# A hybrid encoder layer on one core: pacing of two top-k searches, earlier attention logits, FFN products on another engine

## The chip, the cores and the metric

The kernel runs on one core of a Trainium2 chip. Its time is the device time of one execution in microseconds (us). A core has TensorE (PE, matrix products and transposes into PSUM), VectorE (DVE), ScalarE (ACT), GpSimd (POOL, no access to PSUM) and SyncE (SP), which here only issues transfers. Each engine works through its own instruction list in order and waits on semaphores of the others.

## The reference

One layer of a trunk on x of 2048 rows x 1024, all in float32, with three groups of heads between two norms and a gated FFN behind them:

```python
h = rmsnorm(x, g1)
p = h @ w_in
hA = mlstm_chunkwise(...)
hB = rglru(causal_conv4(lx)) * gelu(lg)
hC = dsa_attention(q, k, v, iq, ik, iw)
x = x + rmsnorm(concat(hA, hB, hC) @ w_out, g2)
u = causal_conv3(rmsnorm(x, g3) @ ffn_up)
gate, up = split(u)
x = x + rmsnorm((gelu(gate) * up) @ ffn_down, g4)
```

In `dsa_attention` an indexer scores every admissible key for every query, the 256 highest are kept, and four heads attend to those keys alone.

## The kernel before, in words

**Stages.** Rows go in four blocks of 512 (`b`). The mixer does, block by block, the input projections, the mLSTM, the LRU, and starts the attention. The FFN then goes over the same four blocks, while the attention's later row tiles still run beside it. Inside FFN block b (`ffn`, L1027) the output projection of block b+1 (`out_proj`, L945) stands in front of the last but one group of products; block 0's stands in the mixer.

**Products.** A float32 product is three products of halves: `gemm_t` and `gemm_r` (L254, L270) go over pieces of weights, each a high part `wh` and a remainder `wl`, loaded on SP's queue or made from a raw load on ACT and POOL (L208, L214). Results lie in four PSUM banks `mm`; three banks `sd` serve everything else, one bank `av` the attention's result.

**Order.** PE's order is the program's (a manual schedule), the other engines' instructions are ordered by the framework's own estimate of time. The program holds a clock `self.now` of PE's work (L48). After each chunk of a product `tick` (L95) runs at most one step of the background streams (generators; the number that a step yields is the time until the next is due), in the order norm, gates, lru, mlstm, att, score. `lanes` (L78) runs the steps of two top-k searches: lane 0 takes the even row tiles (128 queries) and counts on DVE, lane 1 the odd ones and counts on ACT, with a few whole-row DVE steps at its beginning, middle and end. A lane's step sets its own next due time: the yielded length x 1.7 (L93). Lane steps have low priority and are kept behind the last marked DVE and ACT instructions (`dmark`, `amark`).

**Search.** `dsa_mask` (L767) looks for the 256th highest score of n = 128(i+1) keys: a 15-step bisection over the upper 16 bits of the score, a 16-step one over the lower, then a mask of additive values. On DVE a step is a count (L705), a comparison (L717) and a candidate update (L719); on ACT it is a sum of signs (L727) and two small activations. A search holds two of four `pl` planes, the finished mask one, so tile i+2's search begins when tile i's attention is over (L81, L929). Scores of tile i also wait for the mask of tile i-2 (L668).

**Attention.** `dsa_att` (L831) has `nch` chunks of 512 keys, one for tiles 0 to 3 up to four for 12 to 15. `scores(h, ci)` loads keys `ks`, makes logits in an `sd` bank, adds the mask and takes the maximum on DVE into `L` (four buffers, L852); with the head's last chunk it scales the maximum (L859) and exponentiates the head's chunks on ACT (L864). `turn` transposes a chunk of `L` on PE (L59) and copies it to `PT` (L875), `values` multiplies it by the values `vs`. `scores` runs one head ahead of `turn`:

```python
for h in range(4):
    for ci in range(nch):
        turn(h, ci)
        if h < 3:
            scores(h + 1, ci)
        ...
        yield 3.5 if ci + 1 < nch else 4.5
```

`need(b)` (L932) runs all steps of the attention up to block b before `out_proj(b)` reads `d_cat`, without other products between them.

**FFN.** 22 pairs of products (gate and up) go in groups `(4, 4, 4, 4, 4, 2)`, in the last block `(4, 4, 4, 5, 5)`. `conv3` (L1014) reads PSUM once on ACT and twice on DVE (L1020) into `cu` (four buffers); then Gelu on ACT, the product on DVE (L1045), its high part on ACT (L1048), the remainder on DVE (L1049). A group's down product (L1073) comes after the next group's first pair; after a group of five and after the last it comes at once.

**Small things.** `row_rstd` (L130) adds the two halves of a sum of squares and scales it on one column (L144, L145). `proj_val` (L395) and `proj_mlstm` (L415) copy projections out of PSUM; those of `v` all on ACT (L400, L437).

Of the kernel before, what the change touches and what calls it, by code (L numbers as in the profile page):

```python
# [21 lines left out]
EPS = 1e-6  # L22
# [15 lines left out]
class Trunk:  # L38
# [39 lines left out]
    def lanes(self, force=None):  # L78
        for n, lane in enumerate(self.lane):
            while lane and (lane[0][1] <= self.now or force == n):  # L80
                if lane[0][2] and self.planes > 2:  # L81
                    break
                self.planes += 2 * lane[0][2]
                lane[0][2] = False
                with ExitStack() as c:
                    c.enter_context(self.tc.issue_after(self.dmark.ins))
                    c.enter_context(self.tc.issue_after(self.amark.ins))
                    c.enter_context(self.tc.high_priority(offset=-LOW))
                    lag = next(lane[0][0], None)
                if lag is None:  # L90
                    lane.pop(0)
                else:
                    lane[0][1] = max(lane[0][1], self.now - 4.0) + lag * LANES[n]  # L93

# [35 lines left out]
    def row_rstd(self, srcs, first=False):  # L130
        nc = self.nc
        n = len(srcs)
        ss = self.sm.tile([128, n, 2], F32, name="ss")
        for i, x in enumerate(srcs):
            for j in range(2):
                if first and j:
                    c = x[:, 512:1024]
                    junk = self.lp.tile([128, T], F32, name="jk", tag="lt")
                    nc.vector.tensor_tensor_reduce(junk, c, c, 1.0, 0.0, OP.mult, OP.add, ss[:, i, 1:2])
                    continue  # L140
                junk = self.sm.tile([128, 512], BF, name="junk", bufs=1)
                nc.scalar.activation(junk, x[:, j * 512:(j + 1) * 512], AF.Square, accum_out=ss[:, i, j:j + 1])
        v = self.sm.tile([128, n], F32, name="var")
        nc.vector.tensor_tensor(v, ss[:, :, 0], ss[:, :, 1], OP.add)  # L144
        nc.vector.tensor_scalar(v, v, 1.0 / D, EPS, OP.mult, OP.add)  # L145
        return self.rsqrt(self.sm, v, [128, n], "rs")

    def norm_load(self, src, b):
# [246 lines left out]
    def proj_val(self, b, h):  # L395
        nc = self.nc
        o = self.gemm_r(self.win((C_AV, 256)), h)
        for i in range(4):
            vt = self.mst.tile([128, 256], F32, name="vt", tag="mst")
            nc.scalar.activation(vt, o[i][:, :256], AF.Copy)  # L400
            nc.scalar.dma_start(self.d_v[:, :, 4 * b + i, :], vt.rearrange("p (h d) -> p h d", h=4))

    def proj_qk(self, b, h, seen=None):
# [11 lines left out]
    def proj_mlstm(self, b, h, nm):  # L415
        nc = self.nc
        for c0, col in ({"o": (C_MO, 772), "q": (C_MQ, 0), "k": (C_MK, 0), "v": (C_MV, 384)}[nm],):
            if nm == "q":
                o = self.gemm_t(self.win((c0, 384)), [128] * 3, h)
                for i in range(3):  # L420
                    t = self.mst.tile([128, T], F32, name="mst")
                    if i % 2:
                        self.dmark = nc.vector.tensor_copy(t, o[i])
                    else:
                        self.amark = nc.scalar.activation(t, o[i], AF.Copy)
                    nc.scalar.dma_start(self.d_q[i * 128:(i + 1) * 128, b * T:(b + 1) * T], t)
                continue
            n = 392 if nm == "o" else 384
            o = self.gemm_r(self.win((c0, n)), h)
            w = 388 if nm == "v" else 384  # L430
            gs = []
            for i in range(4):
                t = self.mst.tile([128, T], F32, name="mst")
                if nm == "v":
                    tv = t[:, :388].rearrange("p (h d) -> p h d", h=MH)
                    nc.gpsimd.memset(tv[:, :, 96:97], 1.0)
                    self.amark = nc.scalar.activation(tv[:, :, 0:96], o[i][:, :384].rearrange("p (h d) -> p h d", h=MH), AF.Copy)  # L437
                elif nm == "o":
                    self.amark = nc.scalar.activation(t[:, :384], o[i][:, :384], AF.Sigmoid)
                    g = self.mst.tile([128, 8], F32, name="mg", bufs=8)  # L440
                    nc.vector.tensor_copy(g, o[i][:, 384:392])
                    gs.append(g)
                elif i % 2:
                    self.dmark = nc.vector.tensor_copy(t[:, :384], o[i][:, :384])
                else:
                    self.amark = nc.scalar.activation(t[:, :384], o[i][:, :384], AF.Copy)
                r0 = b * T + i * 128
                nc.scalar.dma_start(self.d_m[r0:r0 + 128, col:col + w], t[:, :w])
            if nm == "o":
                self.spawn("gates", self.gates(b, gs), 3.0)  # L450
# [258 lines left out]
    def bisect(self, junk, src, n, need, top):  # L709
# [4 lines left out]
        while bit >= 1:  # L714
            cnt = yield from self.count(junk, src, n, c[:, 0:1])
            t = self.small("stp")
            ve.tensor_scalar(t, cnt, need[:, 0:1], -float(bit), OP.is_lt, OP.mult)  # L717
            c2 = self.small("cand")
            ve.scalar_tensor_tensor(c2, t, float(bit // 2), c, OP.add, OP.add)  # L719
            c = c2  # L720
            bit //= 2
            yield 0.4
# [21 lines left out]
    def bisect_act(self, junk, src, n, need, top):  # L744
# [7 lines left out]
        while True:  # L752
# [8 lines left out]
                yield 0.8 + 0.00084 * n  # L761
                continue
            yield 3.0 + 0.00084 * n
            ve.scalar_tensor_tensor(c, t, 0.5, nb, OP.mult, OP.subtract)
            return c

    def dsa_mask(self, i, sc):  # L767
# [8 lines left out]
        count, bisect = (self.count_act, self.bisect_act) if a else (self.count, self.bisect)  # L776
        u = 0.3 + 0.0011 * n
        ve.tensor_copy(hi[:, :n], halves(I16, 1))
        yield u
        c0 = yield from count(lo.bitcast(BF), hi, n, 0.0)  # L780
        neg, m16, need = s1("neg"), s1("m16", I16), s1("need")
        ve.tensor_scalar(neg, c0, float(TOPK), None, OP.is_lt)
        ve.tensor_scalar(m16, neg, -1.0, None, OP.mult)
        ve.tensor_tensor(need, c0, neg, OP.mult)
        ve.tensor_scalar(need, need, -1.0, float(TOPK), OP.mult, OP.add)  # L785
        ve.tensor_scalar(hi[:, :n], hi[:, :n], m16[:, 0:1], None, OP.bitwise_xor)
        yield 0.8 + u
# [5 lines left out]
        ve.tensor_tensor(need2, need, cg, OP.subtract)  # L793
        ve.tensor_scalar(lo[:, :n], halves(U16, 0), mu, None, OP.bitwise_xor)
        yield u
        ve.scalar_tensor_tensor(lo[:, :n], hi[:, :n], F[:, 0:1], lo[:, :n], OP.is_equal, OP.mult)
        yield u
# [4 lines left out]
        ve.tensor_tensor(need3, need2, cg, OP.subtract)  # L802
        ve.tensor_scalar(need3, need3, -BIG, None, OP.mult)
# [5 lines left out]
        yield 0.8  # L809
        ve.tensor_scalar(lt[:, :n], sc[:, :n], tf, -BIG, OP.is_lt, OP.mult)  # L810
        yield u
        ve.tensor_scalar(eq[:, :n], sc[:, :n], tf, -BIG, OP.is_equal, OP.mult)
        yield u
        ve.tensor_tensor_scan(sc[:, :n], eq[:, :n], eq[:, :n], 0.0, OP.add, OP.min)
        yield 0.3 + 0.0013 * n
        ve.scalar_tensor_tensor(eq[:, :n], sc[:, :n], need3[:, 0:1], eq[:, :n], OP.is_lt, OP.mult)
        yield u
# [13 lines left out]
    def dsa_att(self, i):  # L831
# [50 lines left out]
                self.mm(av[p0:p0 + 64, h * 128:(h + 1) * 128], vs[:, k, :], pt[:, k * 128:(k + 1) * 128],  # L882
                        4 * ci + k < 2, 4 * ci + k >= nk - 2)
        yield 4.0
        for ci in range(nch):
            scores(0, ci)
            yield 1.5 if ci + 1 < nch else 4.0
        av = self.ps.tile([128, 512], F32, name="av", bufs=1)
        before = None
        for h in range(4):  # L890
            for ci in range(nch):
                turn(h, ci)
                if h < 3:
                    scores(h + 1, ci)
                if before is not None:
                    values(*before)
                before = h, ci
                yield 3.5 if ci + 1 < nch else 4.5
# [128 lines left out]
    def ffn(self, b, h):  # L1027
# [7 lines left out]
        for p, ng in enumerate(groups):  # L1035
# [4 lines left out]
            for f in range(f0, f0 + ng):  # L1040
# [1 line left out]
                g = self.conv3(o[0], f, b, hb)  # L1042
                u = self.conv3(o[1], FT + f, b, hb)
                nc.scalar.activation(g, g, AF.Gelu_apprx_tanh)
                nc.vector.tensor_tensor(u, g, u, OP.mult)  # L1045
                gh = self.gp.tile([128, T], F32R, name="gh")
                gl = self.gp.tile([128, T], F32R, name="gl")
                nc.scalar.activation(gh, u, AF.Copy)  # L1048
                nc.vector.tensor_tensor(gl, u, gh.bitcast(F32), OP.subtract)  # L1049
                ghi.append(gh)  # L1050
                glo.append(gl)
                if wait:
# [168 lines left out]
```

## Time and profile before

| what | us |
|---|---|
| median of 3 runs (lowest, highest) | 3037.23 (3031.51, 3037.24) |
| the profiled execution | 3032.87 |
| its span, first to last instruction | 3031.1 |
| PE busy | 2792.7 |
| DVE busy | 1707.5 |
| ACT busy | 1640.9 |
| POOL busy | 705.4 |

The profile is one execution; a span is what its instructions cover, the execution's own time lies 1.8 us above it. PE's busy time is the time in which at least one matmul is under way. In lists of waits a row has the engine, the tile that it writes and the line, then who released it, then the total, how often and the longest. `x4` behind a row of a timeline means that four neighbours are merged; the bracket is the engine's idle time before it and who ended that. The granted clock is a share: 1.00 is 2.4 GHz, and a stretch at half of it runs at 1.2 GHz.

### The profile page before, as it was taken

What the parts mean: (1) busy time and instruction counts of PE and PEld (TensorE: products, weight loads), DVE (VectorE), ACT (ScalarE), POOL (GpSimd) and SP (SyncE); (2) the same over time, 40 slices, a digit from 0 to 9 for tenths busy, and PEclk for the clock granted to TensorE, in tenths of its full rate; (3) what the DMA queues carried; (4) which work ended last, traced back from release to release, by engine and by line L of the source; (5) the groups of instructions that cost most, each with busy time, mean ns of one, the idle gap of its engine ahead of it and who ended that gap; (6) DMA issues with size and microseconds to landing.
All of it is one profiled execution on the core that took longest, in us unless ns stands there. A gap on an engine that the chain in (4) does not pass through costs nothing.

```text
span 3031.1 us, 41666 instructions
## 1 busy us (share of the span) xinstructions
PE 2792.7 (92%) x13568; PEld 2250.2 (74%) x13568; DVE 1707.5 (56%) x3530; ACT 1640.9 (54%) x3268; POOL 705.4 (23%) x615
## 2 busy tenths in 40 slices
PE   7898998898787979998998999989999999999998
PEld 6777787787666757766776777767777777788886
DVE  3653475467337774686578864968643333443334
ACT  4695467554675449756874578356683333221112
POOL 4344222111144333434642000131100023010001
PEclk9999999999988989999999999999999999999999
DMA  8768786675556787875876655466666557575554
GB/s 243 216 201 239 232 260 188 202 229 168 167 150 196 239 215 243 272 233 165 291 257 209 194 191 185 153 196 224 203 214 205 179 168 240 169 265 195 189 193 154
DMA packets 493481, 631.36 MB, mean 208 GB/s; under 512 B 83904, under 2 KB 274368, under 8 KB 493264
## 3 DMA queue, kind: packets, MB, share of 16 engines
q1 hardware_dynamic: 451312, 576.20, 60.6%
q10 hardware_dynamic: 41952, 52.51, 5.0%
q8 instruction: 107, 1.75, 0.2%
q14 instruction: 110, 0.90, 0.1%
HBM read 478.94 MB, written 149.59 MB: 207 GB/s over the span
## 4 chain that ended last, share of the span: by engine, by line
PE 47%; DVE 10%; DMA 8%; ACT 7%; issue 3%; POOL 3%; SPq 1%; ACTq 0%; POOLq 0%; DVEq 0%
PE mm L55 41%; DVE pl L705 3%; PE sd L55 2%; PE sd L59 2%; DMA xr<-d_x 2%; ACT pl L727 2%; PE av L55 1%; DMA W<-d_c 1%; DVE cu L1020 1%; DMA xr<-in_x 1%; POOL y L984 1%; DVE cand L719 1%; ACT L L864 1%; ACT wh L208 1%; ACT cu L1018 1%
## 5 line engine op out<-in xcount | busy, mean ns | idle before, releaser
L55 PE MATMUL mm<-hh,wh 128*128 128x512 f32 (+1 forms) x1920 | 781.0, 407 | 14.7 <-ACT fcar L1022 3.8
L55 PE MATMUL mm<-hh,wl 128*128 128x512 f32 (+1 forms) x1920 | 759.2, 395 | 3.4 <-DMA wl<-d_w 2.7
L55 PE MATMUL mm<-hl,wh 128*128 128x512 f32 (+1 forms) x1920 | 759.5, 396 | 0.0
L214 POOL TENSOR_TENSOR wl<-wr,wh 128x512 fp32r<-128x512 f32 (+3 forms) x315 | 413.0, 1320 | 1121.4 <-ACT wh L208 907.6
L1020 DVE SCALAR_TENSOR_TENSOR cu<-mm,fcw,cu 128x511 f32<-128x511 f32 (+1 forms) x352 | 260.8, 747 | 343.5 <-ACT cu L1018 338.3
L55 PEld LDWEIGHTS mm<-hh,wh 128*128 128x128 f32 (+1 forms) x1920 | 365.6, 190 | 109.1 <-issue 20.2
L55 PEld LDWEIGHTS mm<-hh,wl 128*128 128x128 f32 (+1 forms) x1920 | 364.6, 190 | 86.7 <-DMA wl<-d_w 3.1
L55 PEld LDWEIGHTS mm<-hl,wh 128*128 128x128 f32 (+1 forms) x1920 | 365.7, 190 | 71.5 <-issue 0.2
L1018 ACT ACTIVATE cu<-mm,fcb,fcw 128x512 f32<-128x512 f32 x176 | 135.1, 773 | 401.0 <-PE mm L55 375.3
L55 PE MATMUL mm<-wh,gh 128*128 128x512 f32 x684 | 282.4, 413 | 31.5 <-ACT fcar L1022 16.8
L705 DVE TENSOR_SCALAR_CACHE_REDUCE pl<-pl,cand 128x384 bf16<-128x384 int16 (+13 forms) x217 | 306.0, 1410 | 5.2
L727 ACT ACTIVATE pl<-pl,canda 128x512 bf16<-128x512 int16 (+13 forms) x217 | 294.7, 1358 | 19.9 <-DVE needa L785 6.1
L208 ACT ACTIVATE wh<-wr 128x512 fp32r<-128x512 f32 (+3 forms) x356 | 211.6, 605 | 148.0 <-PE mm L55 72.7
L55 PE MATMUL mm<-wl,gh 128*128 128x512 f32 x684 | 274.8, 402 | 1.0 <-POOL wl L214 0.9
L55 PE MATMUL mm<-wh,gl 128*128 128x512 f32 x684 | 274.5, 401 | 1.1 <-DVE gl L1049 1.1
L55 PE MATMUL mm<-wh,hh 128*128 128x384 f32 (+2 forms) x512 | 182.1, 356 | 17.3 <-ACT lg L623 10.2
L55 PEld LDWEIGHTS mm<-wh,gh 128*128 128x128 f32 x684 | 130.7, 191 | 73.3 <-ACT fcar L1022 22.3
L127 POOL TENSOR_TENSOR rsy<-var,nhalf 128x1 f32<-128x1 f32 x64 | 38.6, 608 | 608.4 <-DVE var L145 503.8
L55 PE MATMUL mm<-wh,hl 128*128 128x384 f32 (+2 forms) x512 | 170.9, 334 | 2.5 <-DVE hl L183 2.4
L55 PE MATMUL mm<-wl,hh 128*128 128x384 f32 (+2 forms) x512 | 170.1, 332 | 0.0
L1082 DVE TENSOR_TENSOR y<-mm,y 128x512 f32<-128x512 f32 x144 | 97.5, 688 | 112.1 <-PE mm L55 110.5
L55 PEld LDWEIGHTS mm<-wh,gl 128*128 128x128 f32 x684 | 130.7, 191 | 33.9 <-DVE gl L1049 2.5
(309 smaller groups left out, 4599.7 us busy)
## 6 DMA issues: line engine op xcount, KB each, us to landing
wh<-d_w SPq DMA_DIRECT2D x451, 256.0 KB, 3.4
wl<-d_w SPq DMA_DIRECT2D x451, 256.0 KB, 3.6
d_w<-wh SPq DMA_DIRECT2D x156, 256.0 KB, 3.5
d_w<-wl SPq DMA_DIRECT2D x156, 256.0 KB, 3.4
ks<-d_ak SPq DMA_DIRECT2D x112, 256.0 KB, 3.9
wr<-in_ffn_up SPq DMA_DIRECT2D x176, 128.0 KB, 3.6
wr<-d_cat SPq DMA_DIRECT2D x64, 256.0 KB, 3.3
wr<-in_w_out SPq DMA_DIRECT2D x64, 256.0 KB, 3.1
```

The lines of the kernel that those rows point to most:

```text
L55: self.nc.tensor.matmul(out, a, b, start=start, stop=stop)
L59: self.nc.tensor.transpose(out, x, self.ident if ident is None else ident)
L127: self.pmark = self.nc.gpsimd.tensor_tensor(y, v, c, OP.pow)
L208: nc.scalar.activation(hi[:, :kk * n], raw[:, :kk * n], AF.Copy)
L214: eng.tensor_tensor(lo[:, :kk * n], raw[:, :kk * n], hi[:, :kk * n].bitcast(F32), OP.subtract)
L705: self.nc.vector.tensor_scalar(out[:, :n], src[:, :n], thr, None, OP.is_ge, OP.add, accum_out=cnt)
L719: ve.scalar_tensor_tensor(c2, t, float(bit // 2), c, OP.add, OP.add)
L727: self.nc.scalar.activation(out[:, :n], src[:, :n], AF.Sign, bias=bias, accum_out=s)
L864: ac.activation(L[h, k][:, :w], L[h, k][:, :w], AF.Exp, scale=0.125, bias=nm[:, 0:1], accum_out=sums[:, h, k:k + 1])
L1018: self.amark = nc.scalar.activation(u, ps, AF.Identity, scale=w[:, 2, j:j + 1], bias=self.fcb[:, j:j + 1])
L1020: self.dmark = nc.vector.scalar_tensor_tensor(u[:, d:], ps[:, :T - d], w[:, 2 - d, j:j + 1], u[:, d:], OP.mult, OP.add)
L1082: self.dmark = nc.vector.tensor_tensor(ys[i][:, c], o[i], ys[i][:, c], OP.add)
```

## The change

A step of the search that is DVE's now yields a tuple. In lane 1 such a step also sets back lane 0's due time. Two `tensor_tensor` or `scalar_tensor_tensor` operations on one column become `tensor_scalar` with a pointer scalar (norms, `bisect`, `bisect_act`, `dsa_mask`). Every second copy of `v` goes to DVE. The attention issues the logits up to four chunks ahead of the transposes (two heads at one or two chunks). In FFN blocks 1 to 3 the product and the remainder are POOL's.

```diff
@@ lanes
+                elif isinstance(lag, tuple):
+                    lane[0][1] = max(lane[0][1], self.now - 4.0) + lag[0] * LANES[n]
+                    if n and self.lane[0]:
+                        self.lane[0][0][1] = max(self.lane[0][0][1], self.now - 4.0) + lag[0] * LANES[0]
@@ row_rstd
-        nc.vector.tensor_tensor(v, ss[:, :, 0], ss[:, :, 1], OP.add)
-        nc.vector.tensor_scalar(v, v, 1.0 / D, EPS, OP.mult, OP.add)
+        if n == 1:
+            nc.vector.tensor_scalar(v, ss[:, 0, 0:1], ss[:, 0, 1:2], 1.0 / D, OP.add, OP.mult)
+            nc.vector.tensor_scalar(v, v, EPS, None, OP.add)
...
@@ proj_val (and the same with i % 2 in proj_mlstm for "v")
-            nc.scalar.activation(vt, o[i][:, :256], AF.Copy)
+            if i % 2:
+                self.dmark = nc.vector.tensor_copy(vt, o[i][:, :256])
+            else:
+                self.amark = nc.scalar.activation(vt, o[i][:, :256], AF.Copy)
@@ bisect
-            ve.scalar_tensor_tensor(c2, t, float(bit // 2), c, OP.add, OP.add)
+            ve.tensor_scalar(c2, t, float(bit // 2), c[:, 0:1], OP.add, OP.add)
@@ dsa_mask (all its own steps alike; need, need2, need3 and bisect_act's last step get pointer scalars)
-        yield u
+        yield (u,)
...
@@ dsa_att
-        for ci in range(nch):
-            scores(0, ci)
-            yield 1.5 if ci + 1 < nch else 4.0
+        jobs = [(h, ci) for h in range(4) for ci in range(nch)]
+        ahead = min(4, 2 * nch)
+        for p in range(ahead):
+            scores(*jobs[p])
+            yield 1.5 if p + 1 < nch else 3.0
+        yield 3.0
...
+        for p, (h, ci) in enumerate(jobs):
+            turn(h, ci)
+            if p + ahead < len(jobs):
+                scores(*jobs[p + ahead])
+            if before is not None:
+                values(*before)
+            before = h, ci
+            yield 5.5 if ahead == nch and ci + 1 == nch else 3.5
@@ ffn
-                nc.vector.tensor_tensor(u, g, u, OP.mult)
+                tail = nc.gpsimd if b else nc.vector
+                tail.tensor_tensor(u, g, u, OP.mult)
...
-                nc.vector.tensor_tensor(gl, u, gh.bitcast(F32), OP.subtract)
+                tail.tensor_tensor(gl, u, gh.bitcast(F32), OP.subtract)
```

## Rows read from the trace of the kernel before

**Rows 1.** The page's first part: busy time of each engine, share, instructions.
```profile
PE 2792.7 (92%) x13568; PEld 2250.2 (74%) x13568; DVE 1707.5 (56%) x3530; ACT 1640.9 (54%) x3268; POOL 705.4 (23%) x615
```
**Rows 2.** Stretches: PE, PEld, DVE, ACT, POOL busy, clock, DMA: mixer, FFN blocks 0, 1.
```profile
0.00:1075.00 1075.00, 944.08 (x5002) 787.67 (x5002) 589.16 (x1449) 634.28 (x1316) 333.98 (x323) 0.94 0.69 207
1075.00:1600.00 525.00, 474.82 (x2183) 370.05 (x2181) 364.94 (x658) 379.04 (x770) 224.54 (x165) 0.96 0.77 245
1600.00:2150.00 550.00, 519.17 (x2482) 406.79 (x2482) 404.80 (x777) 326.01 (x630) 62.37 (x53) 0.98 0.59 192
```
**Rows 3.** The longest of PE's waits over the whole span.
```profile
PE sd L59 <- ACT L L864: 35.0, 20, 6.1
PE mm L55 <- ACT fcar L1022: 26.1, 16, 7.9
```
**Rows 4.** The same wait in 90:320, 520:1035, 1140:1695, 1770:2350 (one to four chunks).
```profile
PE sd L59 <- ACT L L864: 5.8, 3, 3.4
PE sd L59 <- ACT L L864: 4.0, 3, 1.9
PE sd L59 <- ACT L L864: 18.5, 7, 6.1
PE sd L59 <- ACT L L864: 6.6, 7, 2.3
```
**Rows 5.** Timeline, PE: two of these stalls by themselves.
```profile
1462.21 0.47 PE L59 MATMUL sd<-ident,L 128*128 128x128 f32 x1 [4.24 <-ACT L L864]
1634.48 1.11 PE L59 MATMUL sd<-ident,L 128*128 128x128 f32 x4 [6.08 <-ACT L L864]
```
**Rows 6.** Timeline, DVE and ACT ahead of the second stall's end.
```profile
1626.51 1.94 DVE L705 TENSOR_SCALAR_CACHE_REDUCE pl<-pl,cand 128x1664 bf16<-128x1664 int16 x1
...
1633.44 0.14 DVE L859 TENSOR_SCALAR nmx<-nmx 128x1 f32<-128x1 f32 x1
...
1633.61 0.72 ACT L864 ACTIVATE L<-L,nmx 128x512 f32<-128x512 f32 x1 [3.13 <-DVE nmx L859]
```
**Rows 7.** Stretches of 6.8 us behind the first and the last such stall.
```profile
172.80:179.60 6.80, 6.76 (x22) 5.21 (x23) 4.96 (x22) 4.13 (x12) 3.60 (x4) 0.58 0.87 286
...
1634.40:1641.20 6.80, 6.72 (x22) 5.52 (x23) 5.90 (x10) 2.58 (x8) 1.52 (x2) 0.63 0.49 134
```
**Rows 8.** By line (min/median/max ns, first to last start): attention's ends, last logits, projection's reads.
```profile
L926 ACT ACTIVATE hc<-sd x16: 357/372/385, 137.8 to 2411.7; 128x256 f32<-128x256 f32 x16
L852 DVE CUSTOM_DVE_ANT_0 L<-sd,pl x16: 679/692/693, 2292.8 to 2374.9; 128x512 f32<-128x512 f32 x16
L205 SPq DMA_DIRECT2D wr<-d_cat x14: 319/320/392, 2460.5 to 2504.4; - x14
```
**Rows 9.** Transfers of the page: KB each, median us from issue to landing.
```profile
wr<-d_cat SPq DMA_DIRECT2D x64, 256.0 KB, 3.3
```
**Rows 10.** The search's small DVE steps: groups, one line, one meeting with POOL.
```profile
L719 DVE SCALAR_TENSOR_TENSOR cand<-stp,cand 128x1 f32<-128x1 f32 x217 | 60.9, 281 | 4.7
L717 DVE TENSOR_SCALAR stp<-cnt,need 128x1 f32<-128x1 f32 x217 | 45.5, 210 | 3.3
L719 DVE SCALAR_TENSOR_TENSOR cand<-stp,cand x217: 135/160/1260, 81.9 to 2105.2; 128x1 f32<-128x1 f32 x109
700.39 1.29 POOL L643 TENSOR_TENSOR li<-li,y 128x512 f32<-128x512 f32 x1 [3.73 <-issue]
...
700.56 1.13 DVE L719 SCALAR_TENSOR_TENSOR cand<-stp,cand 128x1 f32<-128x1 f32 x1
```
**Rows 11.** PE's waits for copies of `v`.
```profile
PE mm L55 <- ACT mst L437: 2.0, 3, 1.1
```
**Rows 12.** The tail on DVE, a POOL operation of its size, PE's stall ending block 1.
```profile
L1045 DVE TENSOR_TENSOR cu<-cu 128x512 f32<-128x512 f32 x88 | 63.1, 717 | 27.8 <-ACT cu L1044 23.5 <-ACT fcar L1022 0.5
L214 POOL TENSOR_TENSOR wl<-wr,wh 128x512 fp32r<-128x512 f32 (+3 forms) x315 | 413.0, 1320 | 1121.4 <-ACT wh L208 907.6
2150.51 0.51 PE L55 MATMUL mm<-wh,gh 128*128 128x512 f32 x1 [3.41 <-ACT gh L1048]
```

More of the change, by code (lines that the diff above doesn't have):

```diff
@@ L143, in row_rstd @@
         v = self.sm.tile([128, n], F32, name="var")
-        nc.vector.tensor_tensor(v, ss[:, :, 0], ss[:, :, 1], OP.add)
-        nc.vector.tensor_scalar(v, v, 1.0 / D, EPS, OP.mult, OP.add)
+        if n == 1:
+            nc.vector.tensor_scalar(v, ss[:, 0, 0:1], ss[:, 0, 1:2], 1.0 / D, OP.add, OP.mult)
+            nc.vector.tensor_scalar(v, v, EPS, None, OP.add)
+        else:
+            nc.vector.tensor_tensor(v, ss[:, :, 0], ss[:, :, 1], OP.add)
+            nc.vector.tensor_scalar(v, v, 1.0 / D, EPS, OP.mult, OP.add)
         return self.rsqrt(self.sm, v, [128, n], "rs")
@@ L399, in proj_val @@
             vt = self.mst.tile([128, 256], F32, name="vt", tag="mst")
[L400 removed]
+            if i % 2:
+                self.dmark = nc.vector.tensor_copy(vt, o[i][:, :256])
+            else:
+                self.amark = nc.scalar.activation(vt, o[i][:, :256], AF.Copy)
             nc.scalar.dma_start(self.d_v[:, :, 4 * b + i, :], vt.rearrange("p (h d) -> p h d", h=4))
@@ L436, in proj_mlstm @@
                     nc.gpsimd.memset(tv[:, :, 96:97], 1.0)
-                    self.amark = nc.scalar.activation(tv[:, :, 0:96], o[i][:, :384].rearrange("p (h d) -> p h d", h=MH), AF.Copy)
+                    src = o[i][:, :384].rearrange("p (h d) -> p h d", h=MH)
+                    if i % 2:
+                        self.dmark = nc.vector.tensor_copy(tv[:, :, 0:96], src)
+                    else:
+                        self.amark = nc.scalar.activation(tv[:, :, 0:96], src, AF.Copy)
                 elif nm == "o":
@@ L763, in bisect_act @@
             yield 3.0 + 0.00084 * n
-            ve.scalar_tensor_tensor(c, t, 0.5, nb, OP.mult, OP.subtract)
+            ve.tensor_scalar(c, t, 0.5, nb[:, 0:1], OP.mult, OP.subtract)
             return c
@@ L783, in dsa_mask @@
         ve.tensor_scalar(m16, neg, -1.0, None, OP.mult)
-        ve.tensor_tensor(need, c0, neg, OP.mult)
+        ve.tensor_scalar(need, c0, neg[:, 0:1], None, OP.mult)
         ve.tensor_scalar(need, need, -1.0, float(TOPK), OP.mult, OP.add)
         ve.tensor_scalar(hi[:, :n], hi[:, :n], m16[:, 0:1], None, OP.bitwise_xor)
-        yield 0.8 + u
+        yield (0.8 + u,)
         mu = m16.bitcast(U16)[:, 0:1]
@@ L792, in dsa_mask @@
         cg = yield from count(lo.bitcast(BF), hi, n, F1[:, 0:1])
-        ve.tensor_tensor(need2, need, cg, OP.subtract)
+        ve.tensor_scalar(need2, need, cg[:, 0:1], None, OP.subtract)
         ve.tensor_scalar(lo[:, :n], halves(U16, 0), mu, None, OP.bitwise_xor)
-        yield u
+        yield (u,)
         ve.scalar_tensor_tensor(lo[:, :n], hi[:, :n], F[:, 0:1], lo[:, :n], OP.is_equal, OP.mult)
-        yield u
+        yield (u,)
         f = yield from bisect(hi.bitcast(BF), lo, n, need2, 1 << 15)
@@ L801, in dsa_mask @@
         cg = yield from count(hi.bitcast(BF), lo, n, f1[:, 0:1])
-        ve.tensor_tensor(need3, need2, cg, OP.subtract)
-        ve.tensor_scalar(need3, need3, -BIG, None, OP.mult)
+        ve.tensor_scalar(need3, need2, cg[:, 0:1], -BIG, OP.subtract, OP.mult)
         ve.tensor_copy(thr[:, 0:1], f)
@@ L808, in dsa_mask @@
         lt, eq = hi.bitcast(BF), lo.bitcast(BF)
-        yield 0.8
+        yield (0.8,)
         ve.tensor_scalar(lt[:, :n], sc[:, :n], tf, -BIG, OP.is_lt, OP.mult)
-        yield u
+        yield (u,)
         ve.tensor_scalar(eq[:, :n], sc[:, :n], tf, -BIG, OP.is_equal, OP.mult)
-        yield u
+        yield (u,)
         ve.tensor_tensor_scan(sc[:, :n], eq[:, :n], eq[:, :n], 0.0, OP.add, OP.min)
-        yield 0.3 + 0.0013 * n
+        yield (0.3 + 0.0013 * n,)
         ve.scalar_tensor_tensor(eq[:, :n], sc[:, :n], need3[:, 0:1], eq[:, :n], OP.is_lt, OP.mult)
-        yield u
+        yield (u,)
         ve.tensor_tensor(lt[:, :n], lt[:, :n], eq[:, :n], OP.add)
@@ L884, in dsa_att @@
         yield 4.0
-        for ci in range(nch):
-            scores(0, ci)
-            yield 1.5 if ci + 1 < nch else 4.0
+        jobs = [(h, ci) for h in range(4) for ci in range(nch)]
[4 more added lines that the diff above has]
+        yield 3.0
         av = self.ps.tile([128, 512], F32, name="av", bufs=1)
         before = None
[L890 to L898, printed above, removed]
+        for p, (h, ci) in enumerate(jobs):
[6 more added lines that the diff above has]
+            yield 5.5 if ahead == nch and ci + 1 == nch else 3.5
         values(*before)
```

## The prediction

> **What bounds the kernel now.** I began with the page's busy line: TensorE (PE) is busy 92% of the 3031.1 us span, no other engine over 56% of it [rows 1]. Then the busy times by stretch, with the granted clock: the mixer leaves PE idle for 131 of its 1075 us, the first FFN block for 50 of 525, the second for 31 of 550 [rows 2]. The clock column is the second loss: 0.94, 0.96 and 0.98 of full speed, (1 - share) x length, is 64 + 21 + 11 us in these three stretches. So PE is the bound, and a change can only win PE's waits and the half-speed time behind them. The list of PE's waits names the largest: transposes of the logits (the `L` tiles) that wait for ACT's exponential, 35.0 us in 20 waits, ahead of 26.1 us for a PSUM bank held by the convolution [rows 3]. PE's order is written by hand, so whatever waits there holds all that is behind it.
>
> I cut the same list at the four sizes of attention (one to four 512-key chunks): 5.8, 4.0, 18.5 and 6.6 us of it [rows 4]. Then two of the stalls by themselves, 4.24 and 6.08 us [rows 5], and in the second what came late: the logits' maximum was scaled on DVE at 1633.44, behind a 1.94 us count of the DVE search that began at 1626.51, and the exponential started at 1633.61 [rows 6]. Last the clock behind the stalls: the 6.8 us after the first and after the last stall of over 2 us with up to three chunks ran at 0.58 and 0.63 [rows 7].
>
> **The change part by part.** *Logits early.* A transpose now comes later after the logits that close its head: for one chunk two steps of 3.5 us instead of one of 4.5 (2.5 us more cover), for two chunks three steps (6 more), for three chunks two steps (2.5 more), for four chunks 5.5 instead of 4.5 (1 more). Taken off the single waits: with one chunk 0.9 us stays, with two nothing, with three 1.7 of the 4.24 and 3.6 of the 6.08 [rows 5], with four about 2. So 35.0 - 8.2 = 27 us is the upper end. The lower is 0: if DVE is late by its whole queue, more cover is used up. I take two thirds, 18, because a wait that goes lets the next stream run into its own. The clock behind these stalls (seven stalls of 2.0 to 6.1 us, (1 - clock) x 6.8 us each) is worth 12 us [rows 7]; two thirds is 8, bounds 0 and 12. The work itself is the same: the same 160 logit chunks, each with its `ks` load on SP's queue, which now go out by up to three steps earlier; two `ks` buffers hold the queue no longer than before, as a load waits for matmuls of two chunks ago.
>
> *Lane push.* Each DVE step of an odd tile's (ACT) search sets the DVE lane's due time back by its own length x 1.7. That keeps both searches from filling DVE at once. No row prices such a pile-up; the nearest shows a single pass of the search, 1.94 us, ahead of the maximum in the 6.08 us stall [rows 6]. I book 10 us, about five such passes that no longer stand in PE's way; bounds 0 and 25 (half of block 0's idle time). The price is lateness. Steps that begin and end an ACT search of 1280 to 1792 keys come to some 4 to 9 planned us, x 1.7 = 7 to 15 us each. Lane and attention form a chain, as tile i+2's search begins when tile i's attention frees its planes: tile 8 slips by 7, tile 10 by 28, tile 12 by 41, tile 14 by about 65 (6 us of it the longer four-chunk attention). The last attention ends at 2411.7 now and the last output projection reads it from 2460.5, so 49 us are free, where I expect tile 15 to end some 60 to 75 late. What is left of it, the last 11 to 26 of the 37 us between its last logits (2374.9) and its end [rows 8], is then issued before the projection with nothing beside it: copies, transposes and products (an estimate of 5 us, eight steps of 0.4 to 0.7), then the store and its read at 3.3 us each [rows 9], 12 in all, and 3 for the clock. I put 15 us on the path; bounds 0 (the slip stays under 49) and 50.
>
> *Pointer scalars.* The candidate update (two one-column SBUF inputs) has a median of 160 ns and a mean of 281: 217 of them carry 26 us of delay [rows 10]. The rows show whose: one of 1.13 us ends with the POOL product that began just before it [rows 10]. Its neighbour, already with a pointer scalar, costs 210 [rows 10], so the swap saves 71 ns x 217 = 15 us of DVE in the search lane, and a little in the norms. On the path I book 0: the lane runs by due times, not by DVE's speed. Bounds: 11 us of DVE more (50 ns x 217, if nothing was blocked) to 26 us less; neither moves PE by over 3.
>
> The Trainium skill (SBUF — State Buffer, Who interferes with whom) says that a VectorE operation with two SBUF inputs and a GpSimd operation that reads SBUF exclude each other, and that the later one blocks wholly. The row agrees (1.13 us against 0.16). By that rule the FFN part speaks against this change, since it puts 132 such POOL operations beside DVE; its rival stands below.
>
> *Evictions.* Half of the 32 copies of `v` go to DVE. PE waited 2.0 us for those of the mLSTM [rows 11]; I book 2, bounds 0 and 3. On DVE they queue behind counts of up to 2 us, which costs nothing while the next product has free banks.
>
> *FFN tail on POOL.* For blocks 1 to 3 the product and the remainder, 0.72 us each on DVE, become POOL operations at 1.32 [rows 12]. 132 of them are 95 us off DVE and 174 us onto POOL, which works only 62 of 550 us in block 1 [rows 2]. Elsewhere the next group's first product covers it; POOL's post-norm additions stand in the same queue and wait for transfers (about the 3.3 us of [rows 9] each), but four `cu` tiles are two convolution pairs, so a tail may be late by more than a whole product before a convolution waits. Uncovered are three ends: the last group of blocks 1 and 2 and the end of block 3. There PE already stands still (3.41 us [rows 12]) and waits 2 x 0.60 = 1.2 us longer: 3.6 us, and 2 for the clock. DVE's relief in block 1 (32 of 405 us) gives back 2. So +3.5; bounds -4 and +10.
>
> **Sum:** -18 - 8 - 10 + 15 + 0 - 2 + 3.5 = -19.5. The profiled execution took 3032.87, which gives 3013; the median of the runs is 4.4 higher, which gives 3018. I forecast 3015 us.
>
> **The rivals.** (a) *No drain:* the slip stays under 49 us, and the waits go in full: -27 - 12 - 10 - 2 + 3.5 = -47, 2985 us. For it: stalls of PE are not in the plan's clock. Against: the pushes add up in a chain without slack. (b) *The wait only moves:* exponentials stay late because the maximum is late on DVE [rows 6], and early logits fill the three `sd` banks that DVE empties; only the push counts, and the drain eats it: -10 - 2 + 15 = +3, within 3031 to 3043. (c) *Slower, by the drain:* it decides from a slip of about 125 us, where half of tile 15's 16 chunks, which take 82 us now [rows 8], and the 37 us behind them are left when the last projection is due. Eight chunks with nothing between them wait for about one transfer each (3.5 us), 28; with the end of the chain, 12, and 10 for the clock 50. The sum is then +15, 3050 us. For it: one late tile delays all later ones. (d) *POOL locks DVE out:* in block 1 44 operations at 1.32 hold DVE for up to 58 us where 32 are taken off, DVE goes from 405 to 431 of 550, and half of block 1's idle time comes again, 15 us: 3030. Against it: 44 x 1.32 us are 11% of block 1, and the convolution's passes read PSUM. By the rule of the Trainium skill named above (SBUF — State Buffer) it would be so only if every operation met one of DVE's. (e) That the push does nothing is possible only where the DVE lane is empty, as in tile 15's end; elsewhere it acts.
>
> **How the numbers follow.** Forecast 0.42, (a) 0.24, (b) 0.12, (c) 0.16, (d) 0.06. About 0.2% (6 us) is what a measurement of this kernel can tell from no change. Faster by more: forecast, (a) and (d), 0.72. The same: (b), 0.12. Slower: (c), 0.16. The forecast's own range, from the two-thirds terms and the drain's 0 to 30, is 2998 to 3030; to hold 8 in 10 it reaches to (a) and (b): 2980 to 3042.
>
> **What would show it.** Right: PE's wait for the exponential under 15 us; fewer low-clock stretches between 1140 and 1700; the last attention's end near the last projection's first read, with a wait of 10 to 20 us in front of it; the stall at the end of block 1 at 4.6 us; the candidate update at 210 ns, no longer spread. Wrong: no such drain, or one of 40 us; PE's waits for PSUM banks or for DVE's maxima grown by what the exponential lost; the mixer, which only the small parts touch, moved by over 15 us.

## The result and the profile after

The changed kernel takes 2996.74 us in the median (four runs, 2987.30 to 3000.26); the kernel before, beside it, 3035.15. The ratio is 0.9868, 95% interval 0.9846 to 0.989: 38 us faster.

The profiled execution took 2987.3 us, 45.6 less than that of before; it is the quickest of the four, 9.4 under their median, so stretches below carry a few us that are this execution's own. Its busy line, from the page's first part, answers to [rows 1]:

```profile
PE 2771.2 (93%) x13568; PEld 2240.9 (75%) x13568; DVE 1619.1 (54%) x3400; ACT 1643.1 (55%) x3256; POOL 898.4 (30%) x747
```

PE does the same 13568 matmuls. DVE has 88 us less to do, POOL 193 more. PE's time without a matmul, counted over the whole timeline in gaps of over 150 ns, went from 229 to 205 us; the time at the lower of the two clock levels (1.2 GHz) from 217.5 to 183.4, and half of that difference, 17 us, is time won. 24 + 17 = 41 of the 45.6 us.

The stretches of [rows 2], at the same cuts (PE, PEld, DVE, ACT, POOL busy, clock, DMA):

```profile
0.00:1075.00 1075.00, 944.28 (x5010) 790.07 (x5012) 565.96 (x1430) 645.40 (x1325) 345.17 (x332) 0.95 0.72 214
1075.00:1600.00 525.00, 496.04 (x2369) 390.81 (x2370) 373.35 (x703) 382.00 (x784) 230.24 (x171) 0.98 0.78 249
1600.00:2150.00 550.00, 523.03 (x2493) 411.38 (x2492) 405.12 (x749) 300.88 (x581) 127.55 (x97) 0.97 0.60 191
```

The same cuts no longer mean the same work, so here are mixer and first FFN block cut at each kernel's own first convolution, before first:

```profile
0.00:1078.00 1078.00, 944.31 (x5002) 787.67 (x5002) 589.16 (x1449) 634.32 (x1317) 333.98 (x323) 0.94 0.69 207
1078.00:1641.00 563.00, 505.67 (x2309) 394.73 (x2310) 401.24 (x730) 394.95 (x805) 232.85 (x173) 0.95 0.75 239
```

and after:

```profile
0.00:1036.30 1036.30, 911.58 (x4862) 765.43 (x4862) 530.83 (x1354) 614.36 (x1269) 333.43 (x323) 0.95 0.71 212
1036.30:1576.20 539.90, 504.93 (x2392) 396.60 (x2392) 394.76 (x750) 404.45 (x823) 232.22 (x172) 0.97 0.78 251
```

The mixer is 42 us shorter, but 140 of its matmuls (5002 - 4862), most of them of the attention and of the scores that the searches read, now run later; PE is busy 33 us less in it for that reason. The first FFN block takes 83 more matmuls and is still 23 us shorter: PE's idle time there falls from 57 to 35 us and the clock rises from 0.95 to 0.97. Blocks 1 and 2, cut in the same way, take the rest of the moved work (41 and 18 matmuls more) and grow from 538 to 552 and from 484 to 491 us.

PE's longest waits over the span (total, how often, longest), and further down the list the exponential:

```profile
PE mm L55 <- ACT fcar L1038: 17.8, 11, 4.5
PE sd L59 <- DMA mt<-d_m: 16.0, 4, 6.8
PE sd L55 <- DMA ks<-d_ak: 13.1, 2, 12.0
PE mm L55 <- ACT gh L1065: 13.0, 3, 6.5
...
PE mm L55 <- ACT lg L638: 5.6, 5, 2.2
...
PE sd L59 <- ACT L L878: 2.7, 3, 1.4
```

The wait for the exponential, 35.0 us in [rows 3], is 2.7; the wait for the convolution's bank fell with it, from 26.1 to 17.8.

### The profile page after: what moved, and what is told of

The parts are those of the page before. It is cut to its first block, busy times and chain, and to the rows that moved or that the text cites. A ratio compares the mean times of both kernels' runs of the same rounds, so it can differ in the third digit from the quotient of the medians.

```text
span 2985.5 us, 41871 instructions
## 1 busy us (share of the span) xinstructions
PE 2771.2 (93%) x13568; PEld 2240.9 (75%) x13568; DVE 1619.1 (54%) x3400; ACT 1643.1 (55%) x3256; POOL 898.4 (30%) x747
## 4 chain that ended last, share of the span: by engine, by line
PE 38%; DVE 5%; ACT 3%; DMA 3%; issue 3%; POOL 2%; SPq 0%; ACTq 0%; POOLq 0%; DVEq 0%
PE mm L55 34%; PE sd L55 2%; DVE pl L720 1%; PE sd L59 1%; PE av L55 1%; DVE cu L1036 1%; DMA xr<-in_x 1%; ACT pl L742 1%; DMA wr<-in_ffn_up 1%; POOL x L1000 1%; POOL y L1000 1%; ACT L L878 1%; DMA d_x<-x 0%; POOL cu L1062 0%; DMA wr<-d_cat 0%
## 5 line engine op out<-in xcount | busy, mean ns | idle before, releaser
L1062 POOL TENSOR_TENSOR cu<-cu 128x512 f32<-128x512 f32 x66 | 95.5, 1448 | 746.9 <-ACT cu L1060 232.2
L707 DVE SCALAR_TENSOR_TENSOR sc<-rt,iwt,sc 128x512 f32<-128x512 f32 (+3 forms) x114 | 91.7, 804 | 126.6 <-ACT rt L702 125.8
```

What stands on the lines that cost most here:

```text
L707: nc.vector.scalar_tensor_tensor(sc[:, c:c + w], r[:, :w], iw, sc[:, c:c + w], OP.mult, OP.add)
L1062: tail.tensor_tensor(u, g, u, OP.mult)
```

## The experiments

The quoted expectations give their theories letters; for the reader it is enough to know these readings. C: the order of the work is so tight that any shift of it moves the time, whatever the shift is for. D: early logits and lane push pay only together, as the one puts several maxima on DVE in a row and the other keeps the two searches from filling DVE just then. The others let one part, or the sum of the parts taken singly, carry the gain. The kernels of one table ran together, with the kernel before beside them; between tables, gains against that kernel are compared (38.4 us for the changed kernel).

### One part at a time

Early logits alone (`only_ahead`) is the kernel before with this:

```diff
...
+        ahead = min(4, 2 * nch)
+        for p in range(ahead):
+            scores(*jobs[p])
...
+            if p + ahead < len(jobs):
+                scores(*jobs[p + ahead])
```

> The kernel before with the attention's early logits alone. Theory A (the early logits carry the gain, through PE's waits for the exponential): 3035 - 27 to 35 for the waits and the clock, 3000 to 3010 us, the wait for the exponential under 8 us. Theory B (the lane push carries it, by a freer DVE): the waits for the exponential turn into waits for sd banks and maxima, 3025 to 3035 us. In either no drain before the last output projection, as lane 0 is not set back: the last attention ends 30 us or more before the projection's first read.

The push alone (`only_push`), with the yielded tuples:

```diff
+                elif isinstance(lag, tuple):
...
+                    if n and self.lane[0]:
+                        self.lane[0][0][1] = max(self.lane[0][0][1], self.now - 4.0) + lag[0] * LANES[0]
```

> The kernel before with the lane push alone (the yielded tuples). Theory A: little gain, 3025 to 3040 us, since the waits for the exponential stay at 25 us or more, and the last attention is late by 50 to 75 us against the projection. Theory B: 3005 to 3015 us, with the waits for the exponential, for banks held by the convolution and for the Gelu's chain all shorter.

The FFN tail alone (`only_pool`):

```diff
+                tail = nc.gpsimd if b else nc.vector
+                tail.tensor_tensor(u, g, u, OP.mult)
...
+                tail.tensor_tensor(gl, u, gh.bitcast(F32), OP.subtract)
```

> The kernel before with the FFN's product and remainder on POOL in blocks 1 to 3, nothing else. By the prediction's own term +3.5 us (3035 to 3042), the three ends of blocks 1 to 3 longer by 1.2 us each. A rival (DVE's relief outweighs the tails): 3025 to 3032 us, all of it in block 1.

Pointer scalars and the copies of `v` (`only_small`):

```diff
+            ve.tensor_scalar(c2, t, float(bit // 2), c[:, 0:1], OP.add, OP.add)
...
+                self.dmark = nc.vector.tensor_copy(vt, o[i][:, :256])
```

> The kernel before with the pointer scalars and the shared copies of v, nothing else. By the prediction's terms -2 us, within 3028 to 3037 us. A rival (the copies also mark DVE and ACT for the lanes, and shift the mixer): over 8 us in either direction, all of it in the mixer.

Measured, with before at 3035.07:

| kernel | us | ratio (95%) | difference |
|---|---|---|---|
| early logits alone | 3041.50 | 1.0021 (1.0005 to 1.0038) | +6.4 |
| push alone | 3035.45 | 1.0001 (0.9983 to 1.002) | +0.4 |
| FFN tail alone | 3036.11 | 1.0011 (0.9995 to 1.0028) | +1.0 |
| small parts alone | 3022.03 | 0.9961 (0.9945 to 0.9977) | -13.0 |

The four add up to -5, the change gives -38. No part carries it, and the early logits, the largest term of the forecast, make the kernel slower by themselves, outside both of the ranges that were expected. The push alone came within theory A's range, the tail alone within that of the prediction's term. The small parts came by size as the rival had it, over 8 us; but only about half of it shows in the mixer, whose end moves from 1078.0 to 1071.3, and the rest in FFN block 0. The waits of the early logits say how they lose it (the same list of early logits alone):

```profile
PE sd L59 <- DMA mt<-d_m: 30.6, 6, 6.6
PE mm L55 <- ACT fcar L1024: 30.4, 16, 10.0
PE mm L55 <- ACT gh L1050: 20.3, 3, 9.3
PE mm L55 <- ACT lg L623: 14.9, 7, 6.4
...
PE sd L59 <- ACT L L864: 6.9, 3, 5.6
```

The exponential itself did what was worked out: 35.0 - 27 = 8.2 us were to stay, 6.9 did. But the mLSTM's transfers, the convolution's banks, the end of a block (`gh`) and the LRU's gates now hold PE longer, with single stalls of 9 and 10 us. That is rival (b)'s title, the wait that only moves, for this part alone. It is not (b)'s mechanism, by which the exponentials stay late.

### One part left out

Each is the changed kernel with one of the edits above reversed: `no_ahead` has the old loop of `dsa_att`, `no_push` the old `lanes`, `no_pool` the tail on DVE. `gap_before` is an edit without aim, the kernel before with the spacing of the background steps changed a little:

```diff
-GAP, EDGE = 1.3, 0.4
+GAP, EDGE = 1.33, 0.4
```

> The changed kernel with the attention as it was before. Theory A (early logits carry the gain): 3020 to 3035 us, PE's wait for the exponential back at 25 us or more. Theory B (the lane push carries it): 2997 to 3010 us, with that wait at 10 to 20 us.

> The changed kernel without the lane push. Theory A: within 10 us of the changed kernel, 2987 to 3005 us, and the last attention ends well before the last projection reads it. Theory B: 3015 to 3030 us.

> The changed kernel with product and remainder on DVE in all FFN blocks. By the prediction's term 3 to 4 us less than the changed kernel, 2990 to 2996 us; a rival (DVE's relief in block 1 matters): 3003 to 3015 us.

> The kernel before with the least gap between two background steps at 1.33 instead of 1.30 planned us, an edit that aims at nothing. Theory C (any edit of the pacing reshuffles the waits): the time moves by 5 to 20 us either way. Theories A and B take such a shift to be under 5 us: 3030 to 3040.

Measured, with before at 3035.33:

| kernel | us | ratio (95%) |
|---|---|---|
| without early logits | 3020.34 | 0.996 (0.9947 to 0.9974) |
| without the push | 3022.89 | 0.9958 (0.9944 to 0.9972) |
| without the FFN tail on POOL | 2994.01 | 0.9872 (0.9857 to 0.9887) |
| spacing 1.33, nothing else | 3033.07 | 0.9998 (0.9982 to 1.0014) |

Without either early logits or the push the kernel falls back to about the gain of the small parts (-13): each is worth some 25 us beside the other (38.4 - 15.0 and 38.4 - 12.4) and nothing alone. So A and B fall both, though each number lies in one of their ranges; without early logits PE's wait for the exponential is 17.0 us, which only B had. Without the tail on POOL the time is within the 2990 to 2996 of the prediction's own term, but the tail is worth nothing that can be told.

C is not tested. With 1.33 in place of 1.30 the program that is built is the same one, instruction for instruction, and its trace has the same 13568 instructions on PE, 3530 on DVE and 3268 on ACT in the same order; so `gap_before` measures only how far two sets of runs of one program lie apart (2.3 us). What bears on C is which order PE works in. Small parts and tail leave PE's order as it was, all 13568 matmuls; early logits and push change it. With both parts three orders were measured, the changed kernel and the two shortened pushes of the last table below, and these gain 38, 34 and 33 us; with one part alone, beside the small parts and the tail, two orders gain 12 and 15. But the three are the same order up to the end of the mixer. That this order of the mixer is a lucky one is not excluded.

How two searches meet is seen in the kernel without the push, at the end of tile 9's search (lane 1). DVE and the two engines behind it, from that kernel's timeline:

```profile
1295.05 0.81 DVE L828 TENSOR_TENSOR pl<-pl 128x1280 bf16<-128x1280 bf16 x1
...
1295.78 1.67 DVE L716 TENSOR_SCALAR_CACHE_REDUCE pl<-pl,cand 128x1408 bf16<-128x1408 int16 x1
...
1298.61 1.68 DVE L716 TENSOR_SCALAR_CACHE_REDUCE pl<-pl,cand 128x1408 bf16<-128x1408 int16 x1
...
1300.84 1.68 DVE L716 TENSOR_SCALAR_CACHE_REDUCE pl<-pl,cand 128x1408 bf16<-128x1408 int16 x1
...
1302.44 2.71 DVE L1032 SCALAR_TENSOR_TENSOR cu<-mm,fcw,cu 128x511 f32<-128x511 f32 x4
1304.53 0.17 ACT L1034 ACTIVATE fcar<-mm 128x2 f32<-128x2 f32 x1 [6.37 <-DVE cu L1032]
...
1304.76 0.80 PE L55 MATMUL mm<-wh,gh 128*128 128x512 f32 x1 [9.68 <-ACT fcar L1034]
```

ACT's passes of the convolution (L1030) begin at 1296.21 and 1297.39, so DVE's could follow from 1297 on. But three counts of the other lane's search (1408 keys, tile 10) stand in between, right behind the last whole-row step of tile 9's. DVE comes to the convolution at 1302.4, the banks are free at 1304.7, and PE, whose next product needs them, stood for 9.68 us. The same search's end in the changed kernel:

```profile
1263.63 2.82 DVE L828 TENSOR_TENSOR_SCAN sc<-pl 128x1280 f32<-128x1280 bf16 x1
...
1266.37 1.60 DVE L720 TENSOR_SCALAR_CACHE_REDUCE pl<-pl 128x1408 bf16<-128x1408 int16 x1
...
1269.27 1.54 DVE L830 SCALAR_TENSOR_TENSOR pl<-sc,need3a,pl 128x1280 bf16<-128x1280 f32 x1
...
1271.46 0.50 PE L55 MATMUL mm<-wh,gh 128*128 128x512 f32 x1 [1.38 <-DVE y L1099]
```

One count of the other lane, and a stall of 1.38 us. That the push does this at that place is not shown: with the push in the mixer only (next section) tile 9's search, which runs from 1115 to 1289 there, sets nothing back, and the stall at its end is still not one of 9 us:

```profile
1288.53 0.51 PE L55 MATMUL mm<-wh,gh 128*128 128x512 f32 x1 [3.04 <-DVE y L1099]
```

Counted over the timelines, DVE works for over 20 us without a pause of 150 ns in 13 stretches of 455 us in all before, in 17 of 601 with early logits alone, in 15 of 499 without the push and in 10 of 286 in the changed kernel. So beside early logits the push shortens them. But they don't follow the gain: early logits and push without the rest, 30 us faster (next section), have 14 of 431, nearly as before, and the kernel without early logits, 15 us faster, 10 of 312.

### The pair, the pointers, and where the push acts

`pair` is early logits and push without the rest, the two diffs above together; `only_ptr` the pointer scalars without the copies. Two more are the changed kernel with the push cut short: in the mixer only (`push_mixer`), and not after tile 11's mask (`push_to_11`).

```diff
-                    if n and self.lane[0]:
+                    if n and self.lane[0] and self.mixing:
```

```diff
-                    if n and self.lane[0]:
+                    if n and self.lane[0] and 11 not in self.mask_at:
```

> Early logits and lane push together, without the small parts and without POOL in the FFN. Theory D (the two work only together: early logits put four maxima on DVE in a row, and the push keeps the two searches from filling DVE just then): 3005 to 3015 us, and with the small parts' 13 us the whole change. Theory E (the parts add up as they measured alone, +6 and 0): 3036 to 3046 us; then the gain needs the small parts as a third.

> The kernel before with the pointer scalars alone, without the shared copies of v. If DVE operations that POOL locked out stood in PE's way: 3020 to 3028 us, most of the 13 us that the small parts gave. By the prediction's term (the lane runs by due times, DVE's speed does not matter): 3032 to 3038 us, and the copies of v give what the small parts gave.

> The changed kernel with the push only while the mixer runs; none in the FFN. If the push acts in FFN block 0, where the ends of tiles 9 and 11's searches meet counts of the DVE lane: stalls of 9 us near these ends come back, 3008 to 3020 us. If the mixer is where it acts: 2990 to 3003 us. The last attention ends earlier against the last projection in either case.

> The changed kernel with the push until tile 11's mask is done; tiles 13 and 15 set nothing back. By the prediction's drain term (15 us in front of the last projection) the drain shrinks and the time falls to 2982 to 2992 us. If the drain costs next to nothing because its work only moves: 2992 to 3002 us.

Measured, with before at 3036.43:

| kernel | us | ratio (95%) |
|---|---|---|
| early logits and push | 3006.46 | 0.9899 (0.9872 to 0.9926) |
| pointer scalars | 3030.73 | 0.9975 (0.9955 to 0.9995) |
| push in the mixer only | 3002.18 | 0.9877 (0.9848 to 0.9905) |
| push up to tile 11's mask | 3003.68 | 0.9891 (0.9866 to 0.9917) |

*The pair* gives -30.0 where its halves give +6.4 and +0.4: that the two pay only together, D's forecast, is shown. D's reason, DVE kept free just as the maxima come, is not: the exponential, which waits for them, costs PE 6.9 us with early logits alone and 3.5 in the pair, and 2.5 in the changed kernel without the push. Pair, small parts and tail then add up: -30 - 13 + 1 = -42, against -38 of the change. In the pair's list of waits, what early logits alone had made longer is shorter again, but for the mLSTM's transfers:

```profile
PE sd L59 <- DMA mt<-d_m: 28.4, 6, 7.7
PE mm L55 <- ACT fcar L1028: 21.5, 12, 4.8
PE mm L55 <- ACT gh L1054: 13.2, 3, 6.5
...
PE sd L59 <- ACT L L868: 3.5, 3, 1.6
```

*Pointer scalars alone* came between the two ranges that were expected, and decide for neither.

*The mixer only* came as expected if the mixer is where the push acts, 2990 to 3003 us; the stalls of 9 us in block 0 did not come back. Its time is not to be told from that of the changed kernel, although no step in the FFN is pushed back. Its stretches, cut as above:

```profile
0.00:1046.10 1046.10, 917.25 (x4862) 770.75 (x4862) 533.60 (x1358) 614.77 (x1268) 332.34 (x323) 0.95 0.69 210
1046.10:1614.50 568.40, 521.19 (x2431) 406.10 (x2432) 410.36 (x763) 412.84 (x834) 229.10 (x172) 0.95 0.74 241
```

Against the changed kernel block 0 is 28 us longer, with 39 more matmuls in it and a clock of 0.95 instead of 0.97; block 1, which has 41 fewer, is 10 us shorter. Block 2 is 9 us shorter with one matmul fewer; what it lacks is most of the drain of the last attention (below). The two mixers differ by 10 us though PE's order in them is the same: so far apart lie single executions (this one is 5.1 us over its median, that of the changed kernel 9.4 under). The kernel without any push, its execution 5.0 over the median, has as many matmuls in the mixer (4860 and 4862):

```profile
0.00:1069.80 1069.80, 921.69 (x4860) 773.12 (x4860) 566.96 (x1407) 617.88 (x1277) 334.55 (x323) 0.94 0.68 205
```

PE is idle there for 148 us, with the push for 129 (1069.8 - 921.7 and 1046.1 - 917.3). By the gains the push of the mixer alone brings 21.8 of the push's 26.0 us (34.2 - 12.4 and 38.4 - 12.4), and the mixers differ by 24 in these two executions; between early logits alone and the pair they differ by 20 (1071.3 and 1051.4). So most of what the push gives comes from the short searches of up to 1024 keys that run in the mixer, and the 4 us that pushes in the FFN may add are within the intervals. The pile-up shown above is not where the gain lies. In the mixer the wait for the LRU's gates goes from 14.7 to 6.0 us; the trace does not show which DVE step holds it, as ACT, POOL and transfers stand in the same chain. That stays open.

*Push up to tile 11* was to do away with the stall at the last projection, and did not (tile 15's attention still ended 11 us behind the last convolution before it). It missed both expected ranges and tells nothing of that stall's price.

## Why the prediction was right, and where it was not

Faster was right, and 2997 lies in the range, but below the forecast's own 2998 to 3030: it lies between the forecast's 3015 and (a)'s 2985, nearer to the latter. That the sum has the right sign is in part luck: its two largest gains, taken from separate waits, turned out to need each other, which the prediction did not see, and both happened to be in the change. Booked were -21 for early logits, push and drain, -2 for the small parts and +3.5 for the tail; measured are -30.0, -13.0 and +1.0. Taken so, the small parts are furthest off. Step by step:

**The bound** holds: PE's work is the same, and 41 of the 45.6 us between the two executions are PE's waits and the low clock behind them. Which waits, the prediction had right for the exponential alone.

**Logits early, -26, and push, -10.** The two were added as if each stood alone; this is the step that failed. Alone they cost 6.4 us and give nothing, together they give 30.0 with the drain already in it; without the drain (9 to 12 us, below) that is an estimate of some 39 to 42 against the 36 booked. The exponential's wait did fall for early logits alone, so the lower end came for another reason than the one given ("if DVE is late by its whole queue, more cover is used up"). It is the reason of the two thirds, "a wait that goes lets the next stream run into its own", that was sized too small: for early logits alone it took the whole 26. That the exponential's wait ends at 2.7 us, below the 8.2 that was to stay, is not the push's doing, as the kernel without the push has 2.5.

The push was sized on a misread row. Between the count of 1.94 us and the scaling at 1633.44 [rows 6] DVE works for 5 us on other things, most of it (4.4 us) six passes of a post-norm, which no push moves:

```profile
1628.38 1.58 DVE L982 SCALAR_TENSOR_TENSOR y<-y,rsy,gpost 128x512 f32<-128x512 f32 x2
...
1632.11 1.40 DVE L982 SCALAR_TENSOR_TENSOR y<-y,rsy,gpost 128x512 f32<-128x512 f32 x2
```

**The drain, +15,** came where it was put. The last `hc` of an attention starts at 2428.5 (2411.7 in [rows 8]), now 20 us behind the last convolution before the projection, where it had been 58 us ahead: a slip of 78 against PE's own order, for 60 to 75 forecast. The stretch around it in the changed kernel:

```profile
2408.00:2436.00 28.00, 21.15 (x128) 15.08 (x128) 7.63 (x22) 14.57 (x29) 5.14 (x4) 0.82 0.24 71
```

28.0 - 21.2 = 6.9 us idle and 0.18 x 28 = 5.0 of clock make 12. It is spread: eight waits of 0.2 to 1.4 us, not one of 10 to 20. The store and its read were not on the path: the projection's reads of `d_cat` begin at 2392.3, ahead of the attention's end, and from 2436 to 2500 PE waits for 0.6 us in all. The kernel with the push in the mixer only gives a second price: its last attention ends 3 us behind that convolution, with one wait of 2.0 us, and its block 2 is 9 us shorter with one matmul fewer (the changed kernel's line first):

```profile
2128.00:2618.80 490.80, 475.03 (x2262) 377.83 (x2261) 184.12 (x368) 254.82 (x476) 131.59 (x97) 0.99 0.62 202
2156.50:2638.70 482.20, 470.48 (x2261) 374.70 (x2260) 170.70 (x352) 230.73 (x443) 128.06 (x100) 1.00 0.62 208
```

These are two single executions, and the price of 9 to 12 us is an estimate. Rival (c) had its slip far too large. Rival (a), no drain and all waits gone, has the wrong reason and is off by 12 us.

**Pointer scalars, 0.** Mis-sized: alone they are worth 5.7 us (interval of the ratio 0.9955 to 0.9995). The row came out as read:

```profile
L734 DVE TENSOR_SCALAR cand<-stp,cand 128x1 f32<-128x1 f32 x217 | 46.1, 212 | 5.4
```

212 ns against 281, none over 217, so none blocked. "The lane runs by due times, not by DVE's speed" is true, and beside the point: in the kernel with pointer scalars alone PE does its instructions in the very order of before. Where its 5.7 us come from is open. That the maxima come sooner is not seen: its profiled execution, 2.5 us over its median, has the exponential's wait longer than the 35.0 of before, and the convolution's bank at 22.7 for 26.1:

```profile
PE sd L59 <- ACT L L867: 43.9, 20, 6.7
```

Of the further 7.3 us of the small parts (13.0 - 5.7) the copies of `v`, booked at 2, may be the cause; they were not run alone, and the two intervals are wide enough to hold the 7.3.

**FFN tail on POOL, +3.5.** Measured +1.0 alone, and a gain 2.9 us larger without it (41.3 for 38.4), both within their intervals: the size held, within what can be told. Its working did not. The three ends were to grow by 1.2 us each, and the first was to be 4.6:

```profile
2092.07 1.27 POOL L1062 TENSOR_TENSOR cu<-cu 128x512 f32<-128x512 f32 x1 [38.98 <-ACT cu L1060]
...
2094.05 0.51 PE L55 MATMUL mm<-wh,gh 128*128 128x512 f32 x1 [3.15 <-ACT gh L1065]
```

It is 3.15, against 3.41 in [rows 12], and the other two 3.32 and 2.70 for 3.75 and 3.23. With the tail back on DVE and PE's order the same they are 2.88, 3.77 and 2.69: the longer product is there, and the ends do not grow by it. Why is not shown. With the tail alone the first was 5.82. The end of block 0, whose tail stays on DVE, went from 3.66 to 6.50 us, which the prediction did not have.

**Rival (d), POOL that locks DVE out,** is in part there, and costs nothing that can be told. The rival forecast 431 us of DVE in 1600 to 2150, and it is 405; but other work stands in that window now. With the tail alone PE's order is that of before and DVE's other work in block 1 is the same, before first:

```profile
1641.10:2179.20 538.10, 515.62 (x2480) 404.18 (x2479) 390.49 (x753) 330.82 (x636) 59.76 (x51) 0.98 0.60 193
1635.70:2178.70 543.00, 517.98 (x2483) 405.75 (x2482) 382.62 (x708) 330.38 (x637) 127.25 (x95) 0.98 0.58 191
```

31 us of DVE were taken off and its busy time fell by 8, so what is left takes 23 us longer, for 58 in the rival. 9 of these are the 50 candidate updates, with a mean of 382 ns for 203; the convolution's passes out of PSUM keep their 747 ns. In the changed kernel, against the one with the tail on DVE, 30 are taken off, DVE falls by 16 (420.5 to 404.6), and what is left takes 14 longer. Of the rival's time, 15 us, the tail alone shows +1.0. The rule of the Trainium skill behind that rival (SBUF — State Buffer, Who interferes with whom), that such POOL operations and a VectorE step with two SBUF inputs shut each other out, agrees with the candidate update: up to 1.26 us with two tensors, never over 217 ns with a pointer scalar.

**What would show it.** The mixer was to move by under 15 us, "only the small parts touch" it. It moved by 42. The sign was wrong in itself: searches up to tile 7's and attentions up to tile 6's run in the mixer, so push and early logits act there, and most of what the push gives lies there. Of the signs of being right, the exponential under 15 us, the late last attention and the candidate update near 210 ns came; the one wait of 10 to 20 us and the 4.6 us did not.

## What to carry to other kernels

Before adding up the parts of a change to a tight order, ask which part uses the room that another makes: here a step issued earlier took away its own wait of 28 us and gave it all back in other waits, until a second part, worth nothing alone, stood beside it. So run the parts singly and in pairs, and read a wait that goes together with those that grow. When the steps of two background streams meet on an engine, that can show in the main engine's waits under other names (a bank, a gate, a transfer). And before an edit serves as a control, see that the program that is built from it is another one.

## What the runs showed that was not expected

At the border from mixer to FFN stands the longest single wait in the changed kernel's list. Timeline, SP, ACT and PE:

```profile
1019.12 12.05 SPq L1015 DMA_DIRECT2D fcb<-in_ffn_conv_b  x1
...
1036.25 1.45 ACT L1034 ACTIVATE cu<-mm,fcb,fcw 128x512 f32<-128x512 f32 x2 [16.39 <-DMA fcb<-in_ffn_conv_b]
1036.38 0.60 SPq L862 DMA_DIRECT2D ks<-d_ak  x1
...
1040.53 0.77 PE L55 MATMUL sd<-ks,aqh 128*128 128x512 f32 x1 [11.96 <-DMA ks<-d_ak]
```

The issue of one small transfer, the bias of the FFN's convolution, holds SP's queue for 12.05 us; the convolution waits for the bias, and the load of keys behind it, with some stores of weights between, goes out at 1036.4, for which PE stands 11.96 us. Before, the same issue took 11.94 us as well (at 1061.27), and PE stood for 4.5, so these two executions differ by 7 us at this place, against the change. Loading this bias earlier was not tried.
